# Moving three things in a transformer layer in float32: where tiles begin in on-chip memory, the order of a rounding step, and the place of the rotary tables

## The chip, the core and the metric

One core of one Trainium2 chip runs the whole layer. The metric is device time in microseconds, from the core's first to its last instruction with what lies around them. Before the change it is 1897.17 us, the median of three runs (1897.16 to 1900.1).

## The reference

```
x = x + 0.5 * swiglu(rmsnorm(x, ffn1_norm), w_gate, w_up, w_down)      # d_model 2048, d_ff 5632, 256 tokens
h = rmsnorm(x, mix_norm);  proj = h @ w_in                             # 6 kinds of heads
rq, rk, aq, ak, iq, ik = rope(each, positions)                         # cos and sin tables from positions
ro = retention(rq, rk, rv) ... * silu(rg)                              # 8 heads
ao = sparse_attention(aq, ak, av, iq, ik, iw)                          # 8 heads, top 64 of 256 keys by index scores
x = x + concat([ro, ao]) @ w_out
x = x + 0.5 * swiglu(rmsnorm(x, ffn2_norm), w_gate, w_up, w_down)
return rmsnorm(x, final_norm)
```

Everything is float32. The weights are read once, and are most of the 359 MB moved.

## The kernel before

**Two roundings of every operand.** TensorE multiplies rounded float32 numbers (fp32r). To keep the accuracy, each operand is cut into hi (the rounded value, written by ScalarE, ACT) and lo (what is left, written by VectorE, DVE), and a product is three matmuls: hi by hi, hi by lo, lo by hi. A weight tile is loaded into `raw` (three buffers, SyncE's queue), and `split` makes `hi` and `lo` of it (line 280 on ACT, line 286 on DVE, five buffers each of 1024 columns). A unit of such work is called a piece here; a weight load of 2048 columns makes two pieces in a plain pair of rows of blocks (kind C) and four in a pair of kind S.

**Kinds C and S.** `wide` multiplies 256 tokens by 256 rows of weights by 1024 columns, as 2 by 2 by 2 blocks. Kind C does 8 block products (24 matmuls of 512 columns). Kind S is a Strassen-Winograd scheme with 7 block products (21 matmuls), for which DVE forms differences of weight blocks (line 272, four of them) and `blocks_of` forms differences of the left blocks (the `sums`, four blocks) beside the blocks as they are (`alone`). The matmuls are issued at line 232, with the left block as the stationary and the weights as the moving operand.

**Stages in order of time** (us in the trace): the first feed-forward network (FFN1), its hidden columns in two parts of six and five chunks: up products of part 0 (about 7 to 276), down products of part 0 (276 to 402, two halves d = 0 and d = 1 of 63 us), up products of part 1 (402 to 627), down products of part 1 (627 to 740); then the input projections, attention and retention (740 to 1075), the output product (1075 to 1165), and FFN2 in the same manner (1165 to the end). In the up products eight pairs make a chunk, in the order S C S C S C C C: three S (63 matmuls) and five C (120), 183 in all. A down half has the pairs S C S C S C S C C C C C in part 0.

**The left operands' tiles.** In up products the left blocks lie in tiles `xg0` to `xg7` and `ext` (pool `one`); in down products and in the output product they lie in tiles of the pool `mid`. In the first chunk of each FFN, which is all C, three of the eight pairs have theirs in `mid` and five in `xg`. Weights lie in `hi` and `lo` (pool `wts`). In the built program `hi`, `lo` and `mid` tiles begin at 32 modulo 512 bytes, and `xg` and `ext` at 416. Blocks inside them are whole multiples of 512 bytes, so the starts of a stationary and a moving block differ by 384 modulo 512 with `xg` and `ext`, and by 0 with `mid`. In the input projections the weights are stationary and `xg` moves (lines 146 and 148), except in `mm_rows` (lines 163 to 165).

**Turning the hidden values.** At the end of a chunk, `sums_of`, `ups` and `hidden` add up the banks and apply silu; in the middle of the following chunk `turn` transposes the result on TensorE (line 560), and `left_pair` makes the left blocks of a down product of it. Of twelve (ten) turned blocks of a part, four are of kind S (one each for the first four chunks), and go through `blocks_of`: copy out of the bank (line 329, ACT), four small operations on DVE (307 to 310), then ACT rounds the sums (312) and the lone blocks (315), and DVE makes lo of the lone blocks (316) and of the sums (321).

**Order of the work.** One loop runs over the pieces. Each engine executes its own instructions in the order of this loop, and the split of a piece is issued four pieces ahead of its matmuls. `after(step, fn)` hangs other work between pieces; a generator's `yield n` puts its next part n pieces later. `tables` (the cos and sin tables of the rotary embedding) is such a generator: it begins two pieces into the up products of part 1, in steps of three pieces, and holds two `mid` tiles of 1024 columns; its last part (the sine on ACT, two sign products on DVE) stands in the down products of part 1, where `ext` is free of left blocks.

Of the kernel before, what the change touches and what calls it, by code (L numbers as in the profile page):

```python
# [19 lines left out]
P = 128  # L20
T = 256
# [29 lines left out]
def layer(ctx: ExitStack, tc: tile.TileContext, a: dict, out: bass.AP):  # L51
    nc = tc.nc
    V, S, G, TE = nc.vector, nc.scalar, nc.gpsimd, nc.tensor

    one = ctx.enter_context(tc.tile_pool(name="one", bufs=1))
    wts = ctx.enter_context(tc.tile_pool(name="wts", bufs=4))
    mid = ctx.enter_context(tc.tile_pool(name="mid", bufs=16))
    tmp = ctx.enter_context(tc.tile_pool(name="tmp", bufs=2))
    psum = ctx.enter_context(tc.tile_pool(name="psum", bufs=1, space=PSUM))
    ctx.enter_context(tc.manual_schedule())  # L60

# [2 lines left out]
    def new(pool, shape, dt=F32, tag=None, bufs=None):  # L64
        count[0] += 1
        kw = {} if bufs is None else {"bufs": bufs}
        return pool.tile(shape, dt, name=f"{tag}_{count[0]}", tag=tag, **kw)

    def half_k(tag, bufs=2):
        return new(tmp, [P, 2, T], F32, tag, bufs)  # L70

    def big(dt=F32, shape=(P, 4, T)):
        return new(mid, list(shape), dt, "mid")


    gains = new(one, [P, 3 * KT + NH], F32, "gains")
    cst = new(one, [P, 4 + NH], F32, "cst")
    x = [new(one, [P, D], F32, f"x{t}") for t in range(2)]
    xg = {}

# [6 lines left out]
    now, marks = [0], {}  # L87
# [16 lines left out]
    def after(step, fn):  # L104
        ends.setdefault(step, []).append(fn)
# [197 lines left out]
    def blocks_of(v, sums, alone):  # L303

        v = v.rearrange("p j (t n) -> p j t n", t=2)
        f = new(tmp, [P, 4, P], F32, "sq")
        V.tensor_tensor(f[:, 0], v[:, 0, 1], v[:, 1, 1], op=OP.add)
        V.tensor_tensor(f[:, 2], v[:, 0, 1], v[:, 0, 0], op=OP.subtract)
        V.tensor_tensor(f[:, 1], f[:, 0], v[:, 0, 0], op=OP.subtract)
        V.tensor_tensor(f[:, 3], v[:, 1, 0], f[:, 1], op=OP.subtract)  # L310
        vt = v.rearrange("p k t n -> p t k n")
        S.activation(sums[:, :, 0], f, AF.Copy)
        if alone.shape[1] == 4:
            a4 = alone.rearrange("p (t k) h n -> p t k h n", t=2)
            S.activation(a4[:, :, :, 0], vt, AF.Copy)  # L315
            V.tensor_tensor(a4[:, :, :, 1], vt, a4[:, :, :, 0].bitcast(F32), op=OP.subtract)  # L316
        else:
            for o, w in ((slice(0, 2), vt[:, 0]), (slice(2, 3), vt[:, 1, 1:2])):
                S.activation(alone[:, o, 0], w, AF.Copy)
                V.tensor_tensor(alone[:, o, 1], w, alone[:, o, 0].bitcast(F32), op=OP.subtract)  # L320
        V.tensor_tensor(sums[:, :, 1], f, sums[:, :, 0].bitcast(F32), op=OP.subtract)
        return sums, alone

    def left_pair(kind, v, in_psum=True):

        if kind == "S":
            if in_psum:
                f = half_k("b")
                S.activation(f, v, AF.Copy)
                v = f  # L330
            return blocks_of(v, big(F32R, (P, 4, 2, P)), big(F32R, (P, 4, 2, P)))
        t = big(F32R, (P, 2, 512))
        S.activation(t[:, :, :T], v, AF.Copy)
        V.tensor_tensor(t[:, :, T:], v, t[:, :, :T].bitcast(F32), op=OP.subtract)
        return t
# [18 lines left out]
    def s_of_x(c, norm, xT):  # L354
        v = half_k("b")
        for j in range(2):
            S.activation(v[:, j], xT[:, j], AF.Copy, scale=gain(norm, c, j))
        xs[c] = blocks_of(v, new(one, [P, 4, 2, P], F32R, f"xg{c}"), x_ext(c))
# [12 lines left out]
    ext = {}  # L371
# [7 lines left out]
    def mix_ext():  # L379
        t = new(one, [P, EXT], F32, "ext")  # L380
        at = 0
        for name, n in (("rot", 4 * T), ("avw", 2 * W_AV), ("ikT", T), ("score0", P), ("score1", T)):
            ext[name] = t[:, at:at + n]
            at += n
        ext["rot"] = ext["rot"].rearrange("p (k t) -> p k t", k=4)
        ext["avw"] = ext["avw"].rearrange("p (t n) -> p t n", t=2)
        ext["x"] = None
# [27 lines left out]
    def rsqrt(o, v, n):  # L415

        q = new(tmp, [P, 2 * NH], F32, "rs_q", 1)[:, :n]
        S.activation(q, v, AF.Sqrt)
        V.reciprocal(o, q)
        V.scalar_tensor_tensor(q, o, -0.5, o, op0=OP.mult, op1=OP.mult)  # L420
        V.tensor_tensor(q, q, v, op=OP.mult)
        V.scalar_tensor_tensor(o, q, 1.5, o, op0=OP.add, op1=OP.mult)

    def act_table(fn):

        t = new(tmp, [P, 1], F32, "table", 1)
# [15 lines left out]
    def rstd_tok(norm, ts=slice(0, 2)):  # L442
        v = new(tmp, [P, 2], F32, "sum_v", 1)[:, ts]
        s, k = squares[norm]
        V.tensor_reduce(v, s[:, ts, :k[ts.start]], axis=AX.X, op=OP.add)
        V.tensor_scalar(v, v, 1.0 / D, EPS, op0=OP.mult, op1=OP.add)
        if norm not in r_tok:
            r_tok[norm] = new(one, [P, 2], F32, f"r_tok{norm}")
        rsqrt(r_tok[norm][:, ts], v, ts.stop - ts.start)

    def rstd(norm):
        rstd_tok(norm)
        row = yield from row_of(r_tok[norm])
        r_of[norm] = new(tmp, [P, T], F32, "r", 1)
        S.activation(r_of[norm], row, AF.Copy)
# [182 lines left out]
    inv, sgn, kdec = cst[:, 0:2], cst[:, 2:4], cst[:, 4:4 + NH]  # L638


    def tables(at_sin):
        ang, n = big(), big()
        pi, pf = n[:, 0].bitcast(I32), n[:, 1]
        G.dma_start(pi, bass.AP(tensor=a["pos"].tensor, offset=a["pos"].offset, ap=[[0, P], [1, T]]))
        yield 3
        V.tensor_copy(pf, pi)
        for k in range(2):
            for j in range(2):
                V.tensor_scalar(ang[:, 2 * k + j], pf, inv[:, k:k + 1], None, op0=OP.mult)
        yield 3  # L650
        V.tensor_scalar(n, ang, 1.0 / C_TWO_PI, None, op0=OP.mult)
        yield 3
        for k in range(2):
            V.tensor_scalar(n[:, 2 * k], n[:, 2 * k], 0.25, None, op0=OP.add)
        yield 3
        V.tensor_scalar(n, n, MAGIC, None, op0=OP.add)
        yield 3
        V.tensor_scalar(n, n, MAGIC, None, op0=OP.subtract)
        for c in (C1, C2, C3):
            yield 3  # L660
            V.scalar_tensor_tensor(ang, n, -c, ang, op0=OP.mult, op1=OP.add)
        for k in range(2):
            V.tensor_scalar(ang[:, 2 * k], ang[:, 2 * k], math.pi / 2, None, op0=OP.add)
        yield 3

        V.tensor_scalar(n, ang, 1.0 / C_TWO_PI, MAGIC, op0=OP.mult, op1=OP.add)
        yield 3
        V.tensor_scalar(n, n, MAGIC, None, op0=OP.subtract)
        for c in (C1, C2, C3):
            yield 3  # L670
            V.scalar_tensor_tensor(ang, n, -c, ang, op0=OP.mult, op1=OP.add)
        yield 3
        V.tensor_scalar(ang, ang, PI_DOWN, -PI_DOWN, op0=OP.min, op1=OP.max)
        yield 3
        yield at_sin - now[0]
        mix_ext()
        rot = ext["rot"]
        S.activation(rot, ang, AF.Sin)
        yield 2
        for k in range(2):  # L680
            V.tensor_scalar(rot[:, 2 * k + 1], rot[:, 2 * k + 1], sgn[:, k:k + 1], None, op0=OP.mult)


    def first_squares():
        for t in range(2):
            nc.sync.dma_start(x[t], a["x"][t])
        yield 4
        for t in range(2):
            for c in range(2):
                square_x(0, t, 1024 * c, 1024)  # L690
                yield 1
        rstd_tok(0)

    after(FIRST_SQ, first_squares)
    end = ffn(1, 0, 1, False)
    after(marks[1, 1] + 2, lambda: tables(marks[1, 1, "down"] + 2))


    m0 = len(pieces)
# [355 lines left out]
    n = len(pieces)  # L1055
# [100 lines left out]
```

## Time and profile before

| | |
|---|---|
| three runs, us | 1900.1, 1897.16, 1897.17 (median 1897.17) |
| profiled execution: its time, its span, us | 1896.84, 1895.1 |
| mean granted clock of TensorE | 0.998 |
| TensorE busy | 1862.9 us, 98% |
| VectorE busy | 1646.2 us, 87% |
| ScalarE busy | 1072.9 us, 57% |
| weights and inputs moved | 359.33 MB, mean 190 GB/s |

A busy share of TensorE of 98% does not say that its matmuls follow each other as fast as they can: a matmul counts as busy from its start to its modelled end, and neighbours overlap. What one matmul costs is read from how many of them fit into a stretch, and what holds them up from the chain of waits.

### The profile page before, as it was taken

What the parts mean: (1) busy time and instruction counts of PE and PEld (TensorE: products, weight loads), DVE (VectorE), ACT (ScalarE), POOL (GpSimd) and SP (SyncE); (2) the same over time, 40 slices, a digit from 0 to 9 for tenths busy, and PEclk for the clock granted to TensorE, in tenths of its full rate; (3) what the DMA queues carried; (4) which work ended last, traced back from release to release, by engine and by line L of the source; (5) the groups of instructions that cost most, each with busy time, mean ns of one, the idle gap of its engine ahead of it and who ended that gap; (6) DMA issues with size and microseconds to landing.
All of it is one profiled execution on the core that took longest, in us unless ns stands there. A gap on an engine that the chain in (4) does not pass through costs nothing.

```text
span 1895.1 us, 22782 instructions
## 1 busy us (share of the span) xinstructions
PE 1862.9 (98%) x8643; PEld 1525.0 (80%) x8643; DVE 1646.2 (87%) x2109; ACT 1072.9 (57%) x1351; POOL 5.3 (0%) x14
## 2 busy tenths in 40 slices
PE   9999999999999999999999999999999999999997
PEld 7877788887777787988888888877778888777786
DVE  7899998889999997789865786799999889999998
ACT  7655555545555565656654566555555455555564
POOL 0000000000000000000000000000000000000000
PEclk9999999999999999999999999999999999999999
DMA  8544556545455454545434364545554555445554
GB/s 312 199 178 178 199 197 221 194 173 195 182 201 197 165 212 156 188 164 207 178 137 174 134 222 156 200 178 196 201 200 180 200 200 200 178 181 202 194 180 176
DMA packets 51885, 359.33 MB, mean 190 GB/s; under 512 B 5920, under 2 KB 5920, under 8 KB 9280
## 3 DMA queue, kind: packets, MB, share of 16 engines
q1 hardware_dynamic: 50976, 355.62, 50.7%
q8 instruction: 67, 1.10, 0.2%
q10 hardware_dynamic: 432, 1.08, 0.2%
q0 software_dynamic: 368, 1.19, 0.2%
q14 instruction: 42, 0.34, 0.0%
HBM read 355.76 MB, written 2.10 MB: 189 GB/s over the span
## 4 chain that ended last, share of the span: by engine, by line
PE 75%; DVE 19%; ACT 3%; issue 2%; DMA 0%; SPq 0%; DVEq 0%; ACTq 0%
PE M L232 58%; DVE lo L286 8%; PE M L146 8%; PE M L148 4%; DVE raw L272 3%; DVE e L471 2%; ACT hi L280 1%; DVE s L471 1%; PE M L164 1%; PE M L165 1%; PE M L163 1%; DVE x L468 1%; PE M L560 1%; DVE mid L316 1%; ACT mid L315 1%
## 5 line engine op out<-in xcount | busy, mean ns | idle before, releaser
L280 ACT ACTIVATE hi<-raw 128x1024 fp32r<-128x1024 f32 (+2 forms) x859 | 848.3, 1008 | 567.0 <-DVE raw L272 366.4
L286 DVE TENSOR_TENSOR lo<-raw,hi 128x1024 fp32r<-128x1024 f32 (+2 forms) x859 | 978.3, 1159 | 121.9 <-ACT hi L280 107.9
L232 PE MATMUL M<-hi,xg 128*128 128x512 f32 x2240 | 739.2, 396 | 1.4 <-DVE e L471 1.0
L232 PE MATMUL M<-hi,mid 128*128 128x512 f32 x1690 | 528.2, 391 | 4.1 <-DVE e L986 1.7
L232 PEld LDWEIGHTS M<-hi,xg 128*128 128x128 f32 x2240 | 421.7, 188 | 102.8 <-DVE e L471 5.3
L232 PE MATMUL M<-lo,xg 128*128 128x512 f32 x1120 | 443.6, 396 | 5.8 <-DVE lo L286 5.7
L232 PEld LDWEIGHTS M<-hi,mid 128*128 128x128 f32 x1690 | 317.2, 188 | 73.8 <-DVE e L986 2.1
L232 PE MATMUL M<-lo,mid 128*128 128x512 f32 x845 | 329.5, 390 | 1.5 <-DVE lo L286 1.4
L272 DVE TENSOR_TENSOR raw<-raw 128x512 f32<-128x512 f32 x380 | 262.9, 692 | 12.7
L232 PEld LDWEIGHTS M<-lo,xg 128*128 128x128 f32 x1120 | 211.0, 188 | 60.3 <-DVE lo L286 13.0
L146 PE MATMUL M<-xg,hi 128*128 128x512 f32 x688 | 245.1, 398 | 1.2 <-DVE xg L300 1.1
L232 PEld LDWEIGHTS M<-lo,mid 128*128 128x128 f32 x845 | 158.7, 188 | 35.9 <-DVE lo L286 3.5
L148 PE MATMUL M<-xg,lo 128*128 128x256 f32 x645 | 182.1, 282 | 0.0
L146 PEld LDWEIGHTS M<-xg,hi 128*128 128x128 f32 x688 | 128.3, 188 | 30.4 <-DVE xg L300 1.8
L232 PE MATMUL M<-hi,ext 128*128 128x512 f32 x360 | 143.5, 399 | 1.9
L148 PEld LDWEIGHTS M<-xg,lo 128*128 128x128 f32 x645 | 121.3, 188 | 0.8
L232 PEld LDWEIGHTS M<-hi,ext 128*128 128x128 f32 x360 | 67.8, 188 | 23.2 <-DVE s L471 8.0
L232 PE MATMUL M<-lo,ext 128*128 128x512 f32 x180 | 71.1, 395 | 0.0
L471 DVE TENSOR_TENSOR s<-s,M 128x512 f32<-128x512 f32 x98 | 65.5, 683 | 2.2 <-PE M L232 1.2
L550 ACT ACTIVATE s<-s,r_tok 128x512 f32<-128x512 f32 x40 | 27.1, 720 | 54.6 <-DVE s L471 54.6
L471 DVE TENSOR_TENSOR e<-s,M 128x512 f32<-128x512 f32 x58 | 39.6, 684 | 1.0
L232 PEld LDWEIGHTS M<-lo,ext 128*128 128x128 f32 x180 | 33.9, 188 | 7.4
(175 smaller groups left out, 923.7 us busy)
## 6 DMA issues: line engine op xcount, KB each, us to landing
raw<-in_wgu SPq DMA_DIRECT2D x175, 1024.0 KB, 4.8
raw<-in_wd SPq DMA_DIRECT2D x88, 1024.0 KB, 4.8
raw<-in_w_out SPq DMA_DIRECT2D x16, 1024.0 KB, 4.8
raw<-in_w_iq SPq DMA_DIRECT2D x8, 1024.0 KB, 4.8
raw<-in_w_aq SPq DMA_DIRECT2D x8, 1024.0 KB, 4.8
raw<-in_w_rk SPq DMA_DIRECT2D x8, 1024.0 KB, 4.9
raw<-in_w_rq SPq DMA_DIRECT2D x8, 1024.0 KB, 4.8
raw<-in_w_rv SPq DMA_DIRECT2D x8, 1024.0 KB, 4.8
```

What stands on the lines that cost most here:

```text
L146: TE.matmul(acc, lhsT=hi[:, c:c + P], rhs=r, start=st, stop=sp)
L148: TE.matmul(acc[:, T:], lhsT=lo[:, c:c + P], rhs=r[:, :T], start=False, stop=False)
L163: TE.matmul(o, lhsT=h, rhs=hi[:, i * n:(i + 1) * n], start=st, stop=False)
L164: TE.matmul(o, lhsT=h, rhs=lo[:, i * n:(i + 1) * n], start=False, stop=False)
L165: TE.matmul(o, lhsT=l, rhs=hi[:, i * n:(i + 1) * n], start=False, stop=sp)
L232: TE.matmul(bank[m], lhsT=p["left"](pair, a)[u], rhs=split_of[i][v][:, off:off + 512], start=st, stop=sp)
L272: V.tensor_tensor(r[:, o:o + 512], r[:, a:a + 512], r[:, b:b + 512], op=OP.subtract)
L280: S.activation(hi[:, :p["n"]], raw, AF.Copy)
L286: V.tensor_tensor(lo[:, :p["n"]], raw, hi[:, :p["n"]].bitcast(F32), op=OP.subtract)
L315: S.activation(a4[:, :, :, 0], vt, AF.Copy)
L471: V.tensor_tensor(o, a, b, op=OP.add)
L550: S.activation(u[b], bank[SUM[b]] if plain else u[b], AF.Silu, scale=r_tok[norm][:, t:t + 1])
```

## The change

Three edits.

1. **Layout.** The four small tiles `r_tok` (8 bytes a partition, which take 32 each) are allocated at the start of the pool `one`, ahead of `x0`, and no longer when they are first used, behind `xg7`. So all tiles from `x0` to `xg7` move up by 128 bytes: `xg` and `ext` begin at 32 modulo 512 as `hi`, `lo` and `mid` do. `wts`, `mid` and `tmp` stay where they were.
2. **`blocks_of`.** ACT rounds the lone blocks first, ahead of the four operations on DVE and of the sums; DVE's two lo operations keep their order, lone blocks first.
3. **`tables`.** They are computed beside the down products of part 0 of FFN1, from its piece 6 on, in two halves of 512 columns, each with its own load of the positions, with a step of one piece between most parts, and with the sine right behind the clamp. Each half is stored to DRAM through ACT's queue, and four pieces into the down products of part 1 one load through ACT's queue brings both into `ext`.

```diff
+    dram = ctx.enter_context(tc.tile_pool(name="dram", bufs=1, space=bass.MemoryType.DRAM))
...
     cst = new(one, [P, 4 + NH], F32, "cst")
+    r_tok = {n: new(one, [P, 2], F32, f"r_tok{n}") for n in range(4)}
     x = [new(one, [P, D], F32, f"x{t}") for t in range(2)]
...
+        vt = v.rearrange("p k t n -> p t k n")
+        if alone.shape[1] == 4:
+            a4 = alone.rearrange("p (t k) h n -> p t k h n", t=2)
+            parts = [(vt, a4[:, :, :, 0], a4[:, :, :, 1])]
+        else:
+            parts = [(vt[:, 0], alone[:, :2, 0], alone[:, :2, 1]), (vt[:, 1, 1:2], alone[:, 2:, 0], alone[:, 2:, 1])]
+        for w, hi, lo in parts:
+            S.activation(hi, w, AF.Copy)
         f = new(tmp, [P, 4, P], F32, "sq")
...
         S.activation(sums[:, :, 0], f, AF.Copy)
-        if alone.shape[1] == 4:
-            a4 = alone.rearrange("p (t k) h n -> p t k h n", t=2)
-            S.activation(a4[:, :, :, 0], vt, AF.Copy)
-            V.tensor_tensor(a4[:, :, :, 1], vt, a4[:, :, :, 0].bitcast(F32), op=OP.subtract)
...
+        for w, hi, lo in parts:
+            V.tensor_tensor(lo, w, hi.bitcast(F32), op=OP.subtract)
         V.tensor_tensor(sums[:, :, 1], f, sums[:, :, 0].bitcast(F32), op=OP.subtract)
...
-    def tables(at_sin):
-        ang, n = big(), big()
...
+    def tables():
         for k in range(2):
+            ang, n = half_k("b"), half_k("sq")
+            pi, pf = n[:, 0].bitcast(I32), n[:, 1]
+            G.dma_start(pi, bass.AP(tensor=a["pos"].tensor, offset=a["pos"].offset, ap=[[0, P], [1, T]]))
+            yield 3
+            V.tensor_copy(pf, pi)
...
+            V.tensor_scalar(ang, ang, PI_DOWN, -PI_DOWN, op0=OP.min, op1=OP.max)
+            S.activation(ang, ang, AF.Sin)
+            yield 1
+            V.tensor_scalar(ang[:, 1], ang[:, 1], sgn[:, k:k + 1], None, op0=OP.mult)
+            nc.scalar.dma_start(rot_dram[:, 2 * k:2 * k + 2], ang)
+        act_table(AF.Silu)
+
+    def load_tables():
         mix_ext()
-        rot = ext["rot"]
-        S.activation(rot, ang, AF.Sin)
-        yield 2
-        for k in range(2):
-            V.tensor_scalar(rot[:, 2 * k + 1], rot[:, 2 * k + 1], sgn[:, k:k + 1], None, op0=OP.mult)
+        nc.scalar.dma_start(ext["rot"], rot_dram)
...
-    after(marks[1, 1] + 2, lambda: tables(marks[1, 1, "down"] + 2))
+    after(marks[1, 0, "down"] + 6, tables)
+    after(marks[1, 1, "down"] + 4, load_tables)
```

Where this moves instructions. On ACT, at the first S turn (in the second chunk of FFN1), before: `sq` holds the four sums, `b` the blocks as they are, `mid` the rounded left blocks.

```order
L329 ACTIVATE b_780<-M_5_76 128x512
L312 ACTIVATE mid_782<-sq_784 128x4x128
L315 ACTIVATE mid_783<-b_780 128x4x128
L333 ACTIVATE mid_797<-M_7_78 128x2x256
L280 ACTIVATE hi_800<-raw_713 128x1024
```

The same place now:

```order
L332 ACTIVATE b_786<-M_9_82 128x512
L315 ACTIVATE mid_789<-b_786 128x4x128
L321 ACTIVATE mid_788<-sq_791 128x4x128
L336 ACTIVATE mid_803<-M_11_84 128x2x256
L282 ACTIVATE hi_806<-raw_719 128x1024
```

The rounding of the lone blocks, which needs only the copy `b`, now stands ahead of that of the sums, which needs DVE's four operations. DVE's rows are the same there.

On DVE, in the first half of the down products of part 0, from the end of the first table half's range reduction to its last operation: `b` is the angle, `sq` the scratch tile, `raw` and `lo` are the weights' pieces. These rows now stand where only the `raw` and `lo` rows stood.

```order
L669 SCALAR_TENSOR_TENSOR b_2332<-sq_2333,b_2332 128x512
L288 TENSOR_TENSOR lo_2489<-raw_2357,hi_2488 128x512
L669 SCALAR_TENSOR_TENSOR b_2332<-sq_2333,b_2332 128x512
L288 TENSOR_TENSOR lo_2508<-raw_2420,hi_2507 128x1024
L671 TENSOR_SCALAR b_2332<-b_2332 128x512
L288 TENSOR_TENSOR lo_2520<-raw_2420,hi_2519 128x1024
L674 TENSOR_SCALAR b_2332<-b_2332,cst_75 128x256
L288 TENSOR_TENSOR lo_2537<-raw_2445,hi_2536 128x1024
```

One or two table operations now stand ahead of each piece's lo.

On ACT at the same place, the sine and the store stand between the roundings of three pieces, where only the three `hi` rows stood:

```order
L282 ACTIVATE hi_2507<-raw_2420 128x1024
L672 ACTIVATE b_2332<-b_2332 128x512
L282 ACTIVATE hi_2519<-raw_2420 128x1024
L675 DMA rot_dram_115<-b_2332 128x512
L282 ACTIVATE hi_2536<-raw_2445 128x1024
```

The sine reads what DVE's clamp (line 671) writes, and the store what DVE's sign product (line 674) writes, so ACT's order now ties `hi` of a piece to a DVE operation that stands behind `lo` of the piece ahead of it. No new load of an activation table stands beside the sine.

## Rows read from the trace of the kernel before

**Rows 1.** The page, part 1: busy time of each engine.

```profile
PE 1862.9 (98%) x8643; PEld 1525.0 (80%) x8643; DVE 1646.2 (87%) x2109; ACT 1072.9 (57%) x1351; POOL 5.3 (0%) x14
```

**Rows 2.** The page, part 5: matmuls by operands (out<-moving,stationary; xcount; busy, mean ns of one).

```profile
L232 PE MATMUL M<-hi,xg 128*128 128x512 f32 x2240 | 739.2, 396 | 1.4 <-DVE e L471 1.0
L232 PE MATMUL M<-hi,mid 128*128 128x512 f32 x1690 | 528.2, 391 | 4.1 <-DVE e L986 1.7
...
L232 PE MATMUL M<-lo,xg 128*128 128x512 f32 x1120 | 443.6, 396 | 5.8 <-DVE lo L286 5.7
L232 PE MATMUL M<-lo,mid 128*128 128x512 f32 x845 | 329.5, 390 | 1.5 <-DVE lo L286 1.4
...
L146 PE MATMUL M<-xg,hi 128*128 128x512 f32 x688 | 245.1, 398 | 1.2 <-DVE xg L300 1.1
...
L232 PE MATMUL M<-hi,ext 128*128 128x512 f32 x360 | 143.5, 399 | 1.9
```

**Rows 3.** Windows, TensorE: stretch, us, busy (matmuls), clock, DMA share, GB/s.

```profile
58.00:82.00 24.00, 24.00 (x105) 1.00 0.54 197
278.00:312.00 34.00, 34.00 (x152) 1.00 0.56 203
```

**Rows 4.** Chain that ended last, 1259 to 1330 us, in FFN2: start us, us, what.

```profile
1261.13 23.73 PE M L232 x101
1284.86 0.45 PE M L560 x4
...
1305.62 23.82 PE M L232 x101
```

**Rows 5.** Timeline of ACT at that chunk's S turn: start us, us, instruction, idle before.

```profile
1287.02 0.64 ACT L312 ACTIVATE mid<-sq 128x512 fp32r<-128x512 f32 x1 [1.09 <-DVE sq L310]
1287.56 0.62 ACT L315 ACTIVATE mid<-b 128x512 fp32r<-128x512 f32 x1
1288.08 0.58 ACT L333 ACTIVATE mid<-M 128x512 fp32r<-128x512 f32 x1
1288.56 2.00 ACT L280 ACTIVATE hi<-raw 128x1024 fp32r<-128x1024 f32 x2
```

**Rows 6.** Timeline of DVE at the same place.

```profile
1286.70 0.29 DVE L310 TENSOR_TENSOR sq<-b,sq 128x128 f32<-128x128 f32 x1
1288.21 0.69 DVE L316 TENSOR_TENSOR mid<-b,mid 128x512 fp32r<-128x512 f32 x1 [1.22 <-ACT mid L315]
...
1290.02 1.22 DVE L286 TENSOR_TENSOR lo<-raw,hi 128x1024 fp32r<-128x1024 f32 x1
```

**Rows 7.** Waits of the whole span: us in total, times, longest us.

```profile
DVE mid L316 <- ACT mid L315: 23.2, 19, 1.3
```

**Rows 8.** Windows, the same pieces with tables (FFN1) and without (FFN2): PE, PEld, DVE, ACT.

```profile
412.10:499.33 87.23, 81.81 (x352) 65.02 (x351) 84.45 (x110) 45.14 (x51) 0.00 (x0) 1.00 0.49 181
1569.50:1651.17 81.67, 81.23 (x354) 65.16 (x352) 73.75 (x89) 45.57 (x51) 0.00 (x0) 1.00 0.53 193
```

**Rows 9.** Windows, down products of part 0: all, and the tables' new place.

```profile
275.70:401.50 125.80, 125.80 (x561) 104.23 (x560) 111.01 (x125) 67.43 (x70) 0.54 (x1) 1.00 0.55 202
291.18:349.61 58.43, 58.43 (x264) 48.47 (x263) 51.37 (x59) 30.52 (x33) 0.54 (x1) 1.00 0.55 203
```

**Rows 10.** Groups by form in the down products of part 0: DVE's lo at two widths.

```profile
L286 DVE TENSOR_TENSOR lo<-raw,hi 128x1024 fp32r<-128x1024 f32 x56 | 68.0, 1223 | 11.9 <-ACT hi L280 10.1
...
L286 DVE TENSOR_TENSOR lo<-raw,hi 128x512 fp32r<-128x512 f32 x8 | 5.5, 683 | 0.0
```

**Rows 11.** ACT: the sine (groups, 620 to 700 us), and two DMA issues (timeline).

```profile
L678 ACT ACTIVATE ext<-mid 128x1024 f32<-128x1024 f32 x1 | 1.0, 1043 | 0.0
...
1853.81 0.82 ACTq L618 DMA_DIRECT2D mid<-in_last_gain  x2
```

**Rows 12.** Timelines, second down half: two pieces' lo on DVE; the later one's first use.

```profile
348.39 1.82 DVE L286 TENSOR_TENSOR lo<-raw,hi 128x1024 fp32r<-128x1024 f32 x2
...
352.28 0.39 PE L232 MATMUL M<-lo,mid 128*128 128x512 f32 x1
```

More of the change, by code (lines that the diff above doesn't have):

```diff
@@ L310, in blocks_of @@
         V.tensor_tensor(f[:, 3], v[:, 1, 0], f[:, 1], op=OP.subtract)
-        vt = v.rearrange("p k t n -> p t k n")
         S.activation(sums[:, :, 0], f, AF.Copy)
-        if alone.shape[1] == 4:
-            a4 = alone.rearrange("p (t k) h n -> p t k h n", t=2)
-            S.activation(a4[:, :, :, 0], vt, AF.Copy)
-            V.tensor_tensor(a4[:, :, :, 1], vt, a4[:, :, :, 0].bitcast(F32), op=OP.subtract)
[L317 to L320, printed above, removed]
+        for w, hi, lo in parts:
+            V.tensor_tensor(lo, w, hi.bitcast(F32), op=OP.subtract)
         V.tensor_tensor(sums[:, :, 1], f, sums[:, :, 0].bitcast(F32), op=OP.subtract)
@@ L427, in act_table @@
         S.activation(t, ones[:, 0:1], fn)
-    r_tok, r_of = {}, {}
+    r_of = {}
     def row_of(tok):
@@ L446, in rstd_tok @@
         V.tensor_scalar(v, v, 1.0 / D, EPS, op0=OP.mult, op1=OP.add)
-        if norm not in r_tok:
-            r_tok[norm] = new(one, [P, 2], F32, f"r_tok{norm}")
         rsqrt(r_tok[norm][:, ts], v, ts.stop - ts.start)
@@ L638, in layer @@
     inv, sgn, kdec = cst[:, 0:2], cst[:, 2:4], cst[:, 4:4 + NH]
-    def tables(at_sin):
-        ang, n = big(), big()
[L643 to L646, printed above, removed]
-        for k in range(2):
-            for j in range(2):
[L649 to L652, printed above, removed]
-        for k in range(2):
[L654 to L675, printed above, removed]
-        mix_ext()
-        rot = ext["rot"]
-        S.activation(rot, ang, AF.Sin)
-        yield 2
-        for k in range(2):
-            V.tensor_scalar(rot[:, 2 * k + 1], rot[:, 2 * k + 1], sgn[:, k:k + 1], None, op0=OP.mult)
@@ new lines, in layer @@
+    rot_dram = new(dram, [P, 4, T], F32, "rot_dram")
+    def tables():
+        for k in range(2):
+            ang, n = half_k("b"), half_k("sq")
[3 more added lines that the diff above has]
+            V.tensor_copy(pf, pi)
+            for j in range(2):
+                V.tensor_scalar(ang[:, j], pf, inv[:, k:k + 1], None, op0=OP.mult)
+            yield 1
+            V.tensor_scalar(n, ang, 1.0 / C_TWO_PI, None, op0=OP.mult)
+            V.tensor_scalar(n[:, 0], n[:, 0], 0.25, None, op0=OP.add)
+            yield 1
+            V.tensor_scalar(n, n, MAGIC, None, op0=OP.add)
+            V.tensor_scalar(n, n, MAGIC, None, op0=OP.subtract)
+            for c in (C1, C2, C3):
+                yield 1
+                V.scalar_tensor_tensor(ang, n, -c, ang, op0=OP.mult, op1=OP.add)
+            V.tensor_scalar(ang[:, 0], ang[:, 0], math.pi / 2, None, op0=OP.add)
+            yield 1
+            V.tensor_scalar(n, ang, 1.0 / C_TWO_PI, MAGIC, op0=OP.mult, op1=OP.add)
+            V.tensor_scalar(n, n, MAGIC, None, op0=OP.subtract)
+            for c in (C1, C2, C3):
+                yield 1
+                V.scalar_tensor_tensor(ang, n, -c, ang, op0=OP.mult, op1=OP.add)
+            yield 1
+            V.tensor_scalar(ang, ang, PI_DOWN, -PI_DOWN, op0=OP.min, op1=OP.max)
+            S.activation(ang, ang, AF.Sin)
+            yield 1
+            V.tensor_scalar(ang[:, 1], ang[:, 1], sgn[:, k:k + 1], None, op0=OP.mult)
+            nc.scalar.dma_start(rot_dram[:, 2 * k:2 * k + 2], ang)
+        act_table(AF.Silu)
```

## The prediction

> **What bounds the kernel now.** I read the page's busy shares first, then the matmuls by operands, the windows, the chain of waits, and last the timelines of ACT and DVE at the places that the change touches. TensorE is busy 98% of the span and DVE 87% [rows 1]. The 98% hides that a matmul's cost depends on its tiles: with the left block in `xg` or `ext` one lasts 396 to 399 ns, with it in `mid` 390 or 391 [rows 2], though both stream 512 columns against 128 rows. The spacing agrees, at the same granted clock: in a stretch of up products, all `xg` and `ext`, 24 us count 105 matmuls, and in one of down products, all `mid`, 34 us count 152 [rows 3]. A count takes in the one or two under way at the window's start, so I take two off: 233.0 and 226.7 ns. I use the difference of the means, 5.5 ns, which is the smaller.
>
> The chain in the up products has two parts in each chunk that follows an S turn. From 1261.13 to 1284.86 it is TensorE alone, 101 matmuls; then come four transposes, and from 1285.3 it runs through DVE until TensorE goes on at 1305.62 [rows 4], 20.3 us. A chunk has 183 matmuls, so the other 82 lie beside DVE's part. There DVE is the limit, and a faster matmul gives nothing.
>
> **The layout.** 2240 + 1120 matmuls have their left block in `xg`, 360 in `ext` as hi, and by the rule of two hi to one lo 180 more [rows 2]: 3900 in all. With `xg` and `ext` at 32 modulo 512 they have what `mid` has, a difference of starts of 0, so I price each at 5.5 ns less. The bounds are 0 (the place in the memory makes the difference) and 6.3 ns (the spacing). Sixteen chunks follow an S turn (four in each of four parts), so 16 x 82 matmuls lie beside DVE's part, some 1270 of them with `xg` or `ext` (two such parts end in down products). That leaves 2630 x 5.5 ns = 14.5 us; were none covered by DVE, it would be 21.5. In the projections `xg` is the moving operand; its 688 matmuls of line 146 last 398 ns [rows 2], which gives between 0 and 688 x 7 ns = 4.8 us. Their neighbours of 256 columns have no row to compare, so I take 1. The 192 of lines 163 to 165 at 512 columns give 1.1. Layout: 14.5 + 2.1 = 16.6 us.
>
> Here the Trainium skill speaks against the change. Its page SBUF — State Buffer, section Who interferes with whom, gives TensorE two independent read ports, one for the moving operand and one for the weight load, and says that TensorE and ACT never wait on anyone; by that rule the start of a tile could not matter, and this part would be 0 in place of 16.6. The trace does not agree that all such matmuls cost the same: 396 against 391 ns [rows 2]. Whether the start modulo 512 makes it, or the place, the trace leaves open.
>
> **The order in `blocks_of`.** At an S turn ACT waits 1.09 us for DVE's four operations, then rounds the sums (1287.02), the lone blocks (1287.56), the other turned block (1288.08) and the next piece (1288.56) [rows 5]. DVE ends its four operations at 1286.99, stands 1.22 us until the lone blocks are rounded, and begins the next piece's lo at 1290.02 [rows 6]. With the lone blocks first, they are rounded while ACT would wait. The sums still begin at 1287.02, the other block follows 0.54 later, the next piece 0.48 after that, at 1288.04, and with 1.06 for it (two take 2.00) DVE begins lo at 1289.12. That is 0.9 us earlier, and not the whole 1.22, since ACT's hi is late next. DVE's three operations between (0.6 each from start to start) fit before it. The bounds are 0.5 (one ACT operation fewer in front of hi) and 1.22. The wait occurs 19 times, 23.2 us in all [rows 7]; 16 are in the chain of up products: 16 x 0.9 = 14.4 us. The other three feed the output product, and I leave them out, as I do the six turns of x, together worth about 1 us.
>
> DVE's 20.3 us become 19.4. The 82 matmuls at 227 ns take 18.6, so DVE stays the limit there by 0.8, which is why I count the layout only outside.
>
> **The tables leave the up products.** The same pieces take 87.23 us with the tables and 81.67 without [rows 8]: 5.6 us, all gained. DVE is busy 84.45 - 73.75 = 10.7 us longer there for 21 operations; the other 5.1 are hidden now.
>
> **The tables enter the down products.** DVE is busy 111.01 of 125.80 us there [rows 9], so 14.8 are idle, and TensorE does not wait. But it matters where the new work stands. By the order it goes from behind the 13th piece of the first half (its lo ends at 291.18) to ahead of the 39th, in the second half's first pieces. The work: 10.7 us as above; two sign products, 0.6; eleven operations of 1024 columns cut in two, up to 0.14 each (1.22 against twice 0.68 [rows 10]), 1.4; and a second copy of the positions, 0.2: 12.9 us.
>
> Two detours come on top in each half. The sine waits for the clamp and stands ahead of the next hi on ACT, and DVE's next lo waits for that hi: 0.6 (half of 1.04, and a bit [rows 11]) + 1.0 = 1.6. The store waits for the sign product and stands ahead of the following hi: 0.41 to issue (two take 0.82 [rows 11]) + 1.0 + 0.2 for handing over = 1.6. Together 6.4 for two halves. Behind these instructions wait ACT's hi, DVE's lo and then TensorE; each engine's order is fixed, so DVE has nothing else to do.
>
> From 291.18 to 349.61 DVE has 58.43 - 51.37 = 7.06 us idle [rows 9]. Late as it was with the tables, it still stood 2.8 of 87.2 us [rows 8], so I let 1 remain and 6.1 be filled. DVE is then 12.9 + 6.4 - 6.1 = 13.2 us late when it ends the lo that ends at 349.61 (the two begun at 348.39 end there), and TensorE first reads that at 352.28, 2.7 later [rows 12]. So TensorE waits 10.5 us in all. The bounds are 5 (detours of half that size, 1.5 more filled) and 13 (nothing of the idle time past 5 filled, dearer store). The C pieces behind do not give it back, since TensorE never runs faster.
>
> What else moves lies beside other work: the loads of positions on POOL's queue find tiles that are free long before; the stores (256 KB each) and the load (512 KB) on ACT's queue lie under DMA that is busy 55% here [rows 9], and some 100 us pass before the load's tile is read; without that cover the first rope would wait. SP's queue keeps its order. The sine and two products that leave the last down products give back at most 0.3.
>
> **Sum.** Against the profiled execution, 1896.84 us (1.74 more than its span, 0.33 less than the median): 16.6 + 14.4 + 5.6 - 10.5 = 26.1 us less, **1870.7 us**.
>
> **The rivals.**
> - *The tables hide in the down products.* The idle 14.8 us are more than the work, and TensorE does not wait there now [rows 9]. If ACT's detours fall into DVE's idle time, the 10.5 vanish: 1860.2. Against it: half of that idle time lies outside the stretch in which the work is wanted [rows 9].
> - *The layout does nothing.* What tells `xg` from `mid` may be the place in the memory. Then 14.4 + 5.6 - 10.5 = 9.5 remain: 1887.3. For it: no row has `xg` or `ext` at another start. Against it: the same instruction, shape and weights' tiles, and two numbers that the change makes equal. The rule of the Trainium skill above (SBUF — State Buffer, Who interferes with whom) would end here too.
> - *Slower: equal starts collide in the up products.* If a moving and a stationary tile at one start get in each other's way where DVE and ACT work more, and a matmul lasts 8 ns longer (one and a half times the 5.5), 2630 x 8 = 21 us are lost in place of 16.6 gained: 1908.4. It decides from 9.5 / 2630 = 3.6 ns on. Against it: `mid` has equal starts now and is the fast one [rows 2].
>
> **How the numbers follow.** Forecast 0.60, hidden tables 0.15, layout without effect 0.15, collision 0.03; the remaining 0.07 are mixtures, mostly small gains at the turns with dearer tables. About 0.2% (3.8 us) is what a measurement here tells from no change. Faster by more: 0.60 + 0.15 + 0.15 + 0.03 = 0.93; within: 0.03; slower: 0.04. The range goes from the hidden tables with a little more of the layout (1857) to the layout without effect (1889). The likeliest case alone, with the bounds of its terms, is 1862 to 1879.
>
> **What would show it.** Right: `xg` and `ext` matmuls at 391 ns; DVE's wait at the S turn near zero and the lo behind it 0.9 us earlier; part 1's up products of FFN1 as long as FFN2's; new waits of TensorE for DVE in both down halves of part 0, 10 us in all, with DVE waiting for ACT behind sine and store. Wrong: `xg` still at 396, or these down products still at 126 us.

## The result, and the profile after

The changed kernel takes 1873.38 us (median of four runs, 1871.72 to 1874.1) against 1897.63 us for the kernel before (four runs beside them): a ratio of 0.9868, 95% interval 0.9851 to 0.9885. That is 24.3 us less; forecast were 26.1 less (1870.7 us), with a range of 1857 to 1889. The profiled execution took 1874.1 us with a span of 1872.3.

The page after, busy time of each engine and matmuls by operands (as [rows 1, 2]; line numbers move a little from kernel to kernel: L232 is now L234, L286 is L288, L316 is L323):

```profile
PE 1839.9 (98%) x8643; PEld 1525.5 (81%) x8643; DVE 1647.1 (88%) x2122; ACT 1074.4 (57%) x1353; POOL 5.8 (0%) x15
...
L234 PE MATMUL M<-hi,xg 128*128 128x512 f32 x2240 | 725.9, 390 | 0.0
L234 PE MATMUL M<-hi,mid 128*128 128x512 f32 x1690 | 529.9, 392 | 2.6 <-DVE e L986 1.6
...
L148 PE MATMUL M<-xg,hi 128*128 128x512 f32 x688 | 244.5, 399 | 1.2 <-DVE xg L302 1.2
...
L234 PE MATMUL M<-hi,ext 128*128 128x512 f32 x360 | 141.1, 392 | 0.0
```

With `xg` and `ext` on the left a matmul now lasts what it lasts with `mid`: 390 and 392 ns, where the kernel before had 396 and 399. In the projections (L148) nothing moved. DVE has the same work as before.

Windows after (columns as in [rows 8]: length, then busy us and instructions of PE, PEld, DVE, ACT and POOL, then clock, DMA share and GB/s): the pieces that held the tables, the same pieces in FFN2, the down products of part 0 as a whole, and two stretches of them.

```profile
417.05:496.25 79.20, 78.86 (x353) 64.97 (x351) 73.74 (x89) 45.79 (x51) 0.00 (x0) 1.00 0.54 199
1552.20:1631.40 79.20, 78.84 (x352) 64.94 (x350) 73.74 (x89) 45.75 (x51) 0.00 (x0) 1.00 0.55 199
268.76:406.62 137.86, 130.74 (x560) 105.95 (x559) 124.11 (x161) 67.22 (x73) 0.00 (x0) 0.98 0.51 187
312.00:316.30 4.30, 2.42 (x9) 1.96 (x10) 4.28 (x5) 3.08 (x5) 0.00 (x0) 0.66 0.88 301
316.30:320.20 3.90, 3.90 (x11) 2.99 (x10) 3.85 (x8) 1.39 (x2) 0.00 (x0) 0.50 0.58 225
```

Without tables these up products are as long in FFN1 as in FFN2, 79.20 us (87.23 and 81.67 before, [rows 8]). The down products of part 0 take 137.86 us in place of 125.80 [rows 9]: 12.1 us more. And in the last two rows something new stands: the granted clock falls to 0.50, its lower level of 1.2 GHz, at the end of a wait of TensorE, and stays there from 313.4 to 320.2 us. The trace of the kernel before has no such fall before its last 10 us.

The chain of waits at the S turn of [rows 4], now:

```profile
1248.83 23.19 PE M L234 x101
1272.02 0.87 PE M L561 x8
1272.89 16.62 PE M L234 x72
1289.51 0.03 ACTq L282
1289.54 0.22 issue
1289.76 1.05 ACT hi L282
1290.83 1.24 DVE lo L288
1292.11 23.21 PE M L234 x101
```

The 20.3 us on DVE have gone from it. TensorE is the chain up to 1289.51; only the last 2.6 us, one hi and one lo, still run over ACT and DVE, and there TensorE's matmuls start 0.7 us later than unhindered ones would (1.1 in the kernel before).

ACT and then DVE at that turn (as [rows 5, 6]):

```profile
1272.49 0.60 ACT L332 ACTIVATE b<-M 128x512 f32<-128x512 f32 x1 [0.32 <-PE M L561]
1273.12 0.64 ACT L315 ACTIVATE mid<-b 128x512 fp32r<-128x512 f32 x1
1274.40 0.64 ACT L321 ACTIVATE mid<-sq 128x512 fp32r<-128x512 f32 x1 [0.64 <-DVE sq L320]
```

```profile
1272.21 1.23 DVE L288 TENSOR_TENSOR lo<-raw,hi 128x1024 fp32r<-128x1024 f32 x1 [0.64 <-ACT hi L282]
...
1274.08 0.29 DVE L320 TENSOR_TENSOR sq<-b,sq 128x128 f32<-128x128 f32 x1
1274.29 0.69 DVE L323 TENSOR_TENSOR mid<-b,mid 128x512 fp32r<-128x512 f32 x1
...
1276.50 1.23 DVE L288 TENSOR_TENSOR lo<-raw,hi 128x1024 fp32r<-128x1024 f32 x1
```

The lone blocks are rounded at 1273.12, while DVE forms its sums; DVE's 1.22 us of waiting for them is gone. From its last sum to the lo behind the turn DVE takes 2.42 us (1274.08 to 1276.50), where [rows 6] had 3.32 (1286.70 to 1290.02): the 0.9 us of the forecast.

**Where the time went, stage by stage.** Each stage is taken from the start of its first matmul of `wide` to that of the next stage's. U0.1 is the second chunk of part 0's up products, D0.0 the first half of its down products. "No turn" are the five chunks U0.1, U1.0 (both FFNs) and U1.1 (FFN2), "S turn" the thirteen chunks whose start lies in DVE's part behind an S turn, "tables" are U1.1 and U1.2 of FFN1, where the tables stood. The columns are differences to the kernel before in one profiled execution each, in us; the three in the middle are runs 1 to 4 below.

```
stage (us before)            changed  layout  order   tables  layout
                              kernel   alone  alone    alone  + order
two first chunks    92.84      -1.15   -1.50  +0.08    +2.55   -1.90
no turn (5)        215.26      -5.15   -5.15   0.00     0.00   -5.15
S turn (13)        578.91     -17.89   -6.23 -11.60    -0.35  -17.71
tables (2)          93.48      -8.01   +0.27  -0.84    -5.59   -0.71
D0.0                63.48     +10.18   -0.02  +0.02   +10.50   -0.02
D0.1                62.57      +1.86   -0.01   0.00    +1.87   -0.01
D1.0 (both FFNs)   107.88      -0.56   +0.89  -1.73    -0.15   -0.60
mix, attention, out 485.45     -2.66   -1.62  -1.15    -0.05   -2.86
other down halves  178.26      -0.05   -0.05  +0.02     0.00   -0.04
```

The row "mix, attention, out" begins with D1.1 of FFN1, and the table ends with the last matmul of `wide`. The first chunks vary by some 2 us from one execution to the next (the first loads, and in the tables alone a fall of the clock at 16.2 us); the other rows agree within a few tenths wherever the code is the same.

### The profile page after: what moved, and what is told of

Its sections match the earlier page's. It is cut to its first block, busy times and chain, and to the rows that moved or that the text cites. A ratio compares the mean times of both kernels' runs of the same rounds, so it can differ in the third digit from the quotient of the medians.

```text
span 1872.3 us, 22796 instructions
## 1 busy us (share of the span) xinstructions
PE 1839.9 (98%) x8643; PEld 1525.5 (81%) x8643; DVE 1647.1 (88%) x2122; ACT 1074.4 (57%) x1353; POOL 5.8 (0%) x15
## 4 chain that ended last, share of the span: by engine, by line
PE 85%; DVE 10%; ACT 3%; issue 1%; DMA 0%; ACTq 0%; SPq 0%; DVEq 0%
PE M L234 67%; PE M L148 8%; DVE lo L288 5%; PE M L150 4%; ACT hi L282 2%; DVE raw L274 2%; PE M L561 1%; PE M L166 1%; PE M L167 1%; PE M L165 1%; DVE x L469 1%; DMA raw<-in_wgu 0%; PE M L819 0%; DVE e L472 0%; DVE s L472 0%
## 5 line engine op out<-in xcount | busy, mean ns | idle before, releaser
L288 DVE TENSOR_TENSOR lo<-raw,hi 128x1024 fp32r<-128x1024 f32 (+2 forms) x859 | 977.2, 1159 | 130.3 <-ACT hi L282 114.6
L234 PE MATMUL M<-hi,xg 128*128 128x512 f32 x2240 | 725.9, 390 | 0.0
L234 PE MATMUL M<-hi,mid 128*128 128x512 f32 x1690 | 529.9, 392 | 2.6 <-DVE e L986 1.6
L234 PEld LDWEIGHTS M<-hi,xg 128*128 128x128 f32 x2240 | 420.6, 188 | 86.9 <-ACT hi L282 0.2
L234 PE MATMUL M<-lo,xg 128*128 128x512 f32 x1120 | 437.8, 391 | 5.7 <-DVE lo L288 5.7
L234 PEld LDWEIGHTS M<-hi,mid 128*128 128x128 f32 x1690 | 318.3, 188 | 72.3 <-DVE e L986 2.0
L234 PE MATMUL M<-lo,mid 128*128 128x512 f32 x845 | 330.7, 391 | 4.4 <-DVE lo L288 4.4
L234 PEld LDWEIGHTS M<-lo,xg 128*128 128x128 f32 x1120 | 210.3, 188 | 54.9 <-DVE lo L288 12.3
L148 PE MATMUL M<-xg,hi 128*128 128x512 f32 x688 | 244.5, 399 | 1.2 <-DVE xg L302 1.2
L234 PEld LDWEIGHTS M<-lo,mid 128*128 128x128 f32 x845 | 159.2, 188 | 40.2 <-DVE lo L288 8.0
L148 PEld LDWEIGHTS M<-xg,hi 128*128 128x128 f32 x688 | 128.2, 188 | 31.0 <-DVE xg L302 1.9
L234 PE MATMUL M<-hi,ext 128*128 128x512 f32 x360 | 141.1, 392 | 0.0
L234 PEld LDWEIGHTS M<-hi,ext 128*128 128x128 f32 x360 | 67.5, 188 | 17.1 <-DVE s L472 3.5
L234 PE MATMUL M<-lo,ext 128*128 128x512 f32 x180 | 70.1, 389 | 0.0
L733 ACT ACTIVATE b<-e 64x512 f32<-64x512 f32 (+2 forms) x46 | 28.2, 612 | 20.3 <-DVE e L719 19.8
```

Of the source, the lines that this page charges most:

```text
L148: TE.matmul(acc, lhsT=hi[:, c:c + P], rhs=r, start=st, stop=sp)
L234: TE.matmul(bank[m], lhsT=p["left"](pair, a)[u], rhs=split_of[i][v][:, off:off + 512], start=st, stop=sp)
L288: V.tensor_tensor(lo[:, :p["n"]], raw, hi[:, :p["n"]].bitcast(F32), op=OP.subtract)
L733: S.activation(b[p0:p0 + w], q[p1:p1 + w], AF.Copy)
```

## The experiments

**Runs 1 to 4: each edit alone, and the first two together.** The edits are those of the diff above, applied to the kernel before.

> The kernel before with edit 1 alone. Theory of the prediction (DVE sets the 82 matmuls behind an S turn, so that a faster matmul counts only outside them): 14 chunks gain 0.58 us, the others about 1.0, the projections and the output product 2: 17 us less, about 1880. Rival A (DVE covers nothing, all 183 matmuls of a chunk gain 5.7 ns): 24 us less, about 1874. Rival B (the layout works only together with the order): within 4 us of before.

> The kernel before with edit 2 alone. Theory: DVE's stretch behind each S turn is 0.8 to 0.9 us shorter, 14 to 16 times: 11 to 14 us less, 1883 to 1887. Rival A (DVE covers nothing; what edit 2 gives is only the rest of what these chunks gained): 14 x 0.33 = 5 us less, about 1893.

> The kernel before with edit 3 alone. Theory: 5.6 us less in the up products of part 1, 12 us more in the down products of part 0 as in the changed kernel: 6 us more, about 1904. Rival (the 12 us stem from the faster matmuls of the other two edits, which leave DVE less lead): the tables hide, 4 to 6 us less, about 1892.

> Edits 1 and 2, with the tables in their old place. Theory: the changed kernel less 12 us (tables in the down products) plus 5.6 (tables back in the up products): about 1867, faster than both. Rival (with faster matmuls the tables cost more than 5.6 us in the up products): 1870 to 1873.

Measured against 1897.94 us of before: layout 1884.74 (ratio 0.9931, 0.9918 to 0.9945), 13.2 us less; order 1882.46 (0.9917, 0.9904 to 0.9931), 15.5 less; tables 1904.29 (1.0032, 1.0019 to 1.0044), 6.4 more; layout and order 1869.53 (0.9848, 0.9834 to 0.9861), 28.4 less, which is the sum of the two (28.7) within the noise. So the third edit costs the changed kernel 3.9 us, and leaving it out is better. Against their expectations, the layout came short of the 17 us and the order was just above its 11 to 14; the tables alone came out where the theory had them, so that their rival, that they hide, is out; layout and order fell between its theory (1867) and its rival (1870 to 1873).

In the S-turn chunks the layout alone gives 0.48 us each (0.58 expected where DVE's part is covered, 1.04 where nothing is), in the chunks without a turn 1.03, which is 183 x 5.6 ns. The order gives 0.89 in each of the 13, as expected, and 1.1 more in the output product. Rival A is out on both counts, and so is rival B. Two rows show why. The wait that edit 2 removes (as [rows 7]) in the run with the layout alone, in which it is untouched:

```profile
DVE mid L317 <- ACT mid L316: 23.2, 19, 1.3
```

The chain in FFN2 from 1255 to 1322 us in the run with the order alone; it has no other part:

```profile
1254.88 21.38 PE M L232 x92
1276.25 0.87 PE M L561 x8
1277.12 42.82 PE M L232 x183
1319.95 0.87 PE M L561 x8
1320.82 1.40 PE M L232 x6
```

With the order alone TensorE never waits there: at 232.4 ns a matmul (92 in 21.38 us) it is itself the limit. With the faster matmuls added DVE is ahead again by a little, which is the 0.7 us left in the chain further up.

**Run 5: eight differences of starts in one kernel.** On the kernel with layout and order, with room between the `xg` tiles:

```diff
+    def xtile(c, shape):
+        if c not in pads and c:
+            pads[c] = new(one, [P, 16], F32, f"pad{c}")
+        t = new(one, shape, F32R, f"xg{c}")
...
-            t = new(one, [P, 2, 512], F32R, f"xg{c}")
+            t = xtile(c, [P, 2, 512])
```

> Edits 1 and 2 with the tables in their old place, and 64 bytes of room between the xg tiles, so that xg0 to xg7 begin 0, 64, 128, ... 448 bytes (modulo 512) away from hi and lo: a table of spacing by difference in one run. Known: difference 0 gives 226.7 ns from start to start, 384 gives 232.5. If any difference costs the same, xg0 alone is at 226.7 and all others near 232.5; if the price grows with the difference, there is a slope; if the place of the tile in the memory decides and not its start modulo 512, all eight are alike.

One run took 1877.26 us, between before and layout with order, as a mixture would. The spacing is worked out from the trace, matmul by matmul, with the operands' addresses from the built program: the start of the stationary block less that of the moving one, modulo 512, and the mean from one start to the next where both have the same difference (gaps over 270 ns, waits, left out). All of it is from one execution.

```
difference  tile  spacing ns  one lasts ns  count
  0         xg0     227.9        390.3       473
 64         xg1     233.3        395.7       240
128         xg2     232.3        394.7       506
192         xg3     229.9        392.4       198
256         xg4     229.0        391.4       462
320         xg5     233.3        394.3       200
384         xg6     232.7        395.2       506
448         xg7     229.1        391.8       506
  0         mid     227.0        389.6      2477
```

The eight tiles lie beside each other, and yet they differ. Equal starts are the fastest, but the price is neither one step nor a slope: 64, 128, 320 and 384 cost 5 to 6 ns, 192, 256 and 448 cost 2 to 3. The kernel before had 384, among the dear ones. None of the three patterns expected is the one measured. Place and start change together here; it is run 6 that tells them apart.

**Run 6: equal starts at another place.** On the kernel before, 96 unused floats behind the last tile of the pool `one`, which push `wts` and `mid` to 416:

```diff
+        if not pads:
+            pads.append(new(one, [P, 96], F32, "pad"))
```

> The kernel before with 96 unused floats at the end of the pool of long-lived tiles: xg and ext stay at 416 modulo 512, and hi, lo, mid (and raw) move there too. Theory (the difference of the starts decides): xg and ext matmuls 391 ns, mid still 391, and the time of edit 1 alone, 1885. Rival (the start itself decides, 32 is good and 416 is bad): xg stays at 396, mid rises to 396; 2535 x 5.5 ns = 14 us more, about 1911.

1885.63 us (0.9934, 0.9917 to 0.9950), 12.9 us less than before and within the interval of the layout alone. Its matmuls by operands:

```profile
L232 PE MATMUL M<-hi,xg 128*128 128x512 f32 x2240 | 728.0, 391 | 5.6 <-DVE e L473 5.2
L232 PE MATMUL M<-hi,mid 128*128 128x512 f32 x1690 | 528.4, 391 | 4.5 <-DVE e L988 1.7
```

`xg` gains without having been moved, and `mid` at 416 loses nothing. The difference decides, not the start, and not the place, since `xg` lies where it lay.

**Run 7: the tables without ACT's detours.** On the changed kernel:

```diff
+            yield 1
             S.activation(ang, ang, AF.Sin)
...
-            nc.scalar.dma_start(rot_dram[:, 2 * k:2 * k + 2], ang)
+            G.dma_start(rot_dram[:, 2 * k:2 * k + 2], ang)
```

> The changed kernel with the sine one piece behind the clamp and the store on POOL's queue, so that ACT waits for DVE at neither. Theory (ACT's detours make half of the cost): DVE's two waits of 1.65 and 1.61 us go in each half, TensorE's wait of 3.7 us at the transposes nearly goes, and with it the stretch at half clock (2 us): about 6 us less than the changed kernel, 1867. Rival (DVE's work alone sets the cost): within 1.5 us of 1873.4.

1870.19 us (0.9850 of before, 0.9835 to 0.9865), 3.2 less than the changed kernel: between the two expectations, nearer to neither. D0.0 costs 6.54 us more than before in place of 10.18, D0.1 1.27 in place of 1.86. These rows of the changed kernel show what the detours were, ACT and then DVE and TensorE in D0.0:

```profile
307.27 0.63 ACT L672 ACTIVATE b<-b 128x512 f32<-128x512 f32 x1 [2.76 <-DVE b L671]
307.81 1.04 ACT L282 ACTIVATE hi<-raw 128x1024 fp32r<-128x1024 f32 x1
310.46 0.33 ACTq L675 DMA_DIRECT2D rot_dram<-b  x1
310.89 2.00 ACT L282 ACTIVATE hi<-raw 128x1024 fp32r<-128x1024 f32 x2 [2.04 <-DVE b L674]
312.81 0.58 ACT L477 ACTIVATE s<-M 128x512 f32<-128x512 f32 x1
...
331.74 1.06 ACT L282 ACTIVATE hi<-raw 128x1024 fp32r<-128x1024 f32 x1 [1.66 <-PE M L234]
```

```profile
306.81 0.42 DVE L671 TENSOR_SCALAR b<-b 128x512 f32<-128x512 f32 x1
308.88 1.23 DVE L288 TENSOR_TENSOR lo<-raw,hi 128x1024 fp32r<-128x1024 f32 x1 [1.65 <-ACT hi L282]
310.03 0.35 DVE L674 TENSOR_SCALAR b<-b,cst 128x256 f32<-128x256 f32 x1
311.99 2.36 DVE L288 TENSOR_TENSOR lo<-raw,hi 128x1024 fp32r<-128x1024 f32 x2 [1.61 <-ACT hi L282]
```

```profile
313.44 1.12 PE L561 MATMUL M<-ident,e 128*128 128x128 f32 x4 [3.70 <-ACT s L477]
...
316.76 1.05 PE L234 MATMUL M<-hi,mid 128*128 128x512 f32 x2
```

Clamp, sine, hi, lo: each stands behind the one before on another engine, and DVE waits 1.65 us; sign product, store, hi, lo: another 1.61. Behind the store and two hi stands the copy of a bank (L477, 312.81) that TensorE needs before it may transpose, and TensorE waits 3.70 us. In run 7 that wait is 0.6:

```profile
PE M L561 <- ACT s L477: 0.6, 1, 0.6
```

**Run 8: the tables on GpSimd.** On layout with order, the tables at their old place in the program, with `G` in place of `V` (a multiplication and a subtraction for each of the three-operand steps):

```diff
+        def less(v, c):
+            G.tensor_scalar(w, n, c, None, op0=OP.mult)
+            G.tensor_tensor(v, v, w, op=OP.subtract)
...
-            V.scalar_tensor_tensor(ang, n, -c, ang, op0=OP.mult, op1=OP.add)
+            less(v, c)
```

> Edits 1 and 2, and the tables in their old place, but their range reduction on GpSimd in place of VectorE. Edits 1 and 2 alone: 1869.5. Theory (DVE's 10.7 us of table work make all of what the tables cost there, 7.3 us in the chunks U1.1 and U1.2): these chunks take 42.4 and 43.1 us and the time is about 1862. Rival (GpSimd and VectorE hold each other up at the memory): DVE's instructions last longer while GpSimd works, and the time is 1868 or more.

1869.90 us (0.9851, 0.9837 to 0.9866), the same as with the tables on DVE. The two chunks are as short as forecast (7.3 us less than in layout with order), but GpSimd, which no other engine holds back there, works from 342 to 416 us, in D0.1 and U1.0, and these are 3.0 and 6.0 us longer than in layout with order. DVE's groups by form from 344 to 416 us, first in layout with order, then here:

```profile
L287 DVE TENSOR_TENSOR lo<-raw,hi 128x1024 fp32r<-128x1024 f32 x33 | 40.2, 1222 | 6.9 <-ACT hi L281 5.8
L273 DVE TENSOR_TENSOR raw<-raw 128x512 f32<-128x512 f32 x20 | 13.8, 692 | 0.7
...
L468 DVE SCALAR_TENSOR_TENSOR x<-M,x 128x512 f32<-128x512 f32 x4 | 2.7, 688 | 0.6 <-PE M L233 0.6
```

```profile
L287 DVE TENSOR_TENSOR lo<-raw,hi 128x1024 fp32r<-128x1024 f32 x27 | 44.3, 1675 | 0.5 <-ACT hi L281 0.3
L273 DVE TENSOR_TENSOR raw<-raw 128x512 f32<-128x512 f32 x16 | 17.1, 1071 | 0.5
...
L468 DVE SCALAR_TENSOR_TENSOR x<-M,x 128x512 f32<-128x512 f32 x4 | 2.6, 678 | 0.0
```

A lo lasts 1675 ns in place of 1222, a difference of weight blocks 1071 in place of 692; additions that read one operand from a PSUM bank (688 and 678) stay as they are. The rival holds. The 6.0 us of U1.0 take in a wait of TensorE of 3.04 us and a fall of the clock behind it. The Trainium skill (SBUF — State Buffer, section Who interferes with whom) says that a VectorE instruction with two inputs in SBUF contends with a GpSimd instruction that reads SBUF; these rows agree.

**Runs 9 and 10: the tables beside C pairs.** Each half of the tables begins later, in run 9 on run 7's kernel, in run 10 on the changed kernel:

```diff
         for k in range(2):
+            yield max(0, marks[1, 0, "down"] + 15 + 32 * k - now[0])
             ang, n = half_k("b"), half_k("sq")
```

> The kernel no_detours (1870.2 us) with each half of the tables begun nine pieces later or more, so that it lies beside the run of five C pairs that ends each down half. A C pair gives TensorE 24 matmuls (5.4 us) and DVE two lo of 1.22 us; an S pair 21 matmuls (4.8 us) and about 7 us of DVE. Theory (the place decides: beside S pairs DVE has no time to spare, beside C pairs it has): the two down halves cost 0 to 2 us more than without tables in place of 7.8, so about 1863, 6 to 8 us below no_detours and the fastest of all. Rival (the x additions in the same stretch, 5.4 us, have used that time up): the same cost as no_detours, 1868 to 1870.

> The changed kernel (1873.4 us) with its tables, sine and store as they are, begun at the same pieces as in c_run. Theory (place first, detours second): 2 to 4 us above c_run, 1865 to 1867, so the place is worth 7 us and more, and the detours about 3 as they were beside the S pairs. Rival (the detours cost whatever the place, 6.4 us for both halves): 6 us above c_run.

Run 9: 1863.14 us (0.9813, 0.9799 to 0.9826), where its theory had it; run 10: 1864.51 (0.9819, 0.9806 to 0.9833). In run 9 D0.0 costs 1.70 us more than before and D0.1 nothing. The place is worth 7.1 us without detours and 8.9 with them (1873.38 to 1864.51); the detours cost 3.2 beside S pairs and 1.4 beside C pairs, less than either expectation. In run 10's trace they do not stand in the down halves (1.72 us more than before, 1.69 in run 9) but in U1.0 behind them, which takes 1.4 us longer than in run 9. Run 9 is the fastest kernel, 35 us below before and 10 below the changed one. Windows of its two down halves:

```profile
268.00:331.00 63.00, 61.50 (x276) 50.79 (x276) 61.18 (x80) 34.69 (x37) 0.34 (x1) 1.00 0.55 200
331.00:394.00 63.00, 63.00 (x280) 52.17 (x279) 60.01 (x77) 33.47 (x35) 0.74 (x2) 1.00 0.59 207
```

DVE is busy 61.2 and 60.0 of 63 us, and TensorE stands 1.5 us in all.

## Why the prediction was right, step by step

**The layout: mechanism right, 13.2 us measured alone for 16.6.** The price of 5.5 ns a matmul is what the chunks without a turn show, and DVE's part behind S turns covers the rest as argued. The rivals "the layout does nothing" and "equal starts collide" are out with it. What was mis-sized: the two chunks with the tables, counted among the others, gave nothing (+0.27 where some 1.5 less was due), since faster matmuls only found DVE late there (run 6, whose trace lacks the fall of the clock that run 1 has at that place, gives +0.24, so the clock is not the reason); the thirteen S-turn chunks gave 0.08 each less than taken; and the two D1.0 gave 0.9 back, because a TensorE that comes earlier to a stretch which DVE sets just waits longer. In the projections the gain of edit 1 was 1.6 with the output product, near the 2.1 taken, but not from line 146, whose matmuls stayed at 399 ns; those of lines 163 to 165 with 512 columns fell from 402, 394 and 394 to 397, 390 and 389.

By the rule of the Trainium skill weighed there (SBUF — State Buffer, Who interferes with whom: independent read ports, TensorE waits on no one) this part would have been 0. Runs 1, 5 and 6 disagree with it: 227 ns at equal starts, up to 233 at others.

**The order in `blocks_of`: 15.5 us alone for 14.4.** The sixteen turns gave 14.2 (11.60 + 0.84 + 1.73), 0.89 each; the three turns for the output product, which the forecast left out, gave 1.1. The sentence "DVE stays the limit there by 0.8" leaves out the four further transposes that TensorE does in the same stretch, 0.45 us as the first four [rows 4]. At the old matmul that is enough to turn the limit over (run 2: the chain is TensorE alone). At the new one DVE stays the limit, as forecast, and by 0.7 us: an S-turn chunk is that much longer than one without a turn.

**The tables leave the up products: 5.6 us alone, as forecast, but 7.3 in company.** With the faster matmuls the tables cost more at their old place (layout with order against the changed kernel: -0.71 and -8.01), because the time that hid 5.1 us of them had become shorter. One thing could have passed for this: the trace of layout and order has a fall of the clock at that place (470.2 to 473.6 us), and that of the kernel before has none. Counted matmul by matmul against the kernel without tables there, it is not the reason: the waits up to the transposes of U1.1 and at them cost 5.8 us in company and 4.1 alone, and what follows costs 1.5 in both, in company at the lower clock, alone in waits for lo.

**The tables enter the down products: +12.0 us for +10.5.** The two detours were forecast at 1.6 us each and stand in the trace at 1.65 and 1.61 in the first half and at 1.65 each in the second. The lower bound of 5 us is 5.8 by its own terms (10.5 less 3.2 for half the detours and 1.5); the measured time lies within either. Three things about the step were not as it put them. First, it made one sum over both halves, settled at the end of the second; in fact DVE had caught up between them (at 331.74, in the row shown with run 7, hi waits 1.66 us for a buffer that TensorE frees, so the splits are as far ahead as the buffers let them), so that the first half paid 10.2 and the second 1.9. Second, the longest wait is not at a lo with its 2.7 us of lead but at transposes that need ACT's copy of a bank, which has no lead. Third, the clock fell at the end of that wait, a term that the forecast did not have. The matmuls from 313.4 to 320.2 us took 3.6 us longer than the same ones in the kernel before (eight transposes, a wait of 0.45 us, and nine matmuls at 427 ns from start to start in place of 227, 1.8 us). So the waits themselves made 8.4 of the 12.0 us, less than the 10.5 forecast. The rival that the tables hide fails where they were put, and holds where run 9 puts them, but for 1.7 us; its argument, idle time of DVE, was sound, and so was the objection that the idle time lay elsewhere.

**The sum.** 13.2 + 15.5 - 6.4 = 22.3 us from the edits alone, 24.3 together: the 2 us between are the tables' dearer stay in faster up products. The errors of the terms, 3.4 us too much for the layout and 1.5 too little for the tables' cost, were partly made good by 1.1 more from the order and 1.7 more from the tables' leaving. That the total came within 1.8 us of the forecast is to that extent luck.

What stays open: why differences of 192, 256 and 448 cost less than 64, 128, 320 and 384; and why a matmul of 512 columns that is followed by one of 256, as in the projections, gains nothing from equal starts.

## What to carry to other kernels

Look at the matmul's mean by operands: where equal shapes last differently, compare the starts of the stationary and the moving tile, and try equal ones; a few unused bytes in a pool do it. Before work is moved into "idle" time of an engine, find the pairs or pieces in which that idle time lies, and make no other engine's queue wait for the result (issue the store from an idle queue, the function one step later). When two edits act on the same stretch, run each alone and both: here two added up to within 0.3 us and the third was a loss that the others hid.

## What the runs showed of the hardware

- **A matmul's spacing depends on where its two operands begin relative to each other**: 227 ns at equal starts modulo 512 bytes, 229 to 230 at 192, 256 and 448, 232 to 233 at 64, 128, 320 and 384, for 512 columns at the full clock (run 5; equal starts also in the kernel before, the changed kernel and run 6).
- **The clock fell behind some waits of TensorE**, to 0.50, and 5 to 9 matmuls followed each other at 427 ns: behind 3.70 us in the changed kernel and 3.69 in the tables alone, 3.04 in run 8, 2.61 to 2.83 in runs 1, 2, 4 and 5 (beside the tables at their old place), and in run 7 behind five shorter ones (0.57 to 1.18 us, between 300 and 312 us). A wait of 2.65 us at that old place in the kernel before and one of 2.82 in run 6 were not followed by it, nor were single waits of 1.4 to 1.7 us elsewhere, the 1.50 us of runs 9 and 10 among them. So the length of a wait alone does not tell. The lower clock cost about 1.5 us more than the wait in run 4 and about 3 in the changed kernel.
- **GpSimd at work makes VectorE's instructions with two operands in SBUF longer by 37 to 55%** (1222 to 1675 and 692 to 1071 ns), so that here the idle GpSimd was no free place for elementwise work beside a busy VectorE.
